# A gated linear-recurrence and retention layer: long gated units in two parts, and the forward forget logits made in the pair products

## The chip, the cores and the metric

The kernel runs on one core of one Trainium2 chip. The metric is device time in microseconds (us) of one execution. The engines are TensorE (PE: matmuls, with weight loads shown as PEld), VectorE (DVE), ScalarE (ACT), GpSimd (POOL) and SyncE (SP, which issues transfers). Each works through its own queue in the order of the program, and waits on semaphores of the others.

## The reference

Two inputs, 512 and 1024 rows of width 1024, pass through the same layer. It projects, runs two kinds of two-way recurrence in chunks, gates, projects again and normalises:

```
u    = x * (1 + scale) + shift                # from silu(c) @ w_ada
proj = u @ w_in                               # aq, af_f, af_b, ai, ag | rq, rk, rv, rg
q_a = silu(aq) * 128**-0.5 ; v_a = ai
forget(fl): logf = logaddexp(log_lb, log1m_lb + log_sigmoid(fl)); kk = (1 - lb) * sigmoid(-fl)
o_a = hgrn2(q_a, k_f, logf_f, v_a) + flip(hgrn2(flipped q_a, k_b, logf_b, v_a))   # 8 heads of 128
y_a = rms_norm(o_a) * a_norm_w * silu(ag)
o_r = retention forward + flipped retention   # 8 heads, rope on q and k
y_r = layer_norm(o_r) * silu(rg)
g_a, g_r = split(sigmoid(u @ w_mg + b_mg))
s   = (g_a * (y_a @ w_pa) + g_r * (y_r @ w_pb)) @ w_out
out = layer_norm(ALPHA * x + (1 + gate) * s) * ln_g + ln_b
```

## The kernel before, in words

Every long product is made of three matmuls per block of 128 rows of u, since each fp32 operand is split into a high and a low part in a faster format: ACT copies the high part of a weight block, DVE subtracts for the low part (lines 104 and 113, class `Stream`, which also loads the raw blocks through SP's queue in the order of a list). `gemm_f` (line 364) makes a [128 x 512] result of 24 matmuls of 512 columns, `gemm_t` (line 375) a [128 x 256] one of 24 matmuls of 256 columns.

The short input (512 rows, group 0) comes first, then the long one (group 1). Work goes by units. A gated unit (kind A) of group 1 is one head with two lanes (its two halves of 512 rows), and there are eight; four rotary units (kind R) follow. For a gated unit, `pre_A` makes the products for q and the two forget logits, `mid_A` those for values and gates, and `stages_A` returns a list of short pieces: a first level and levels h = 1, 2, 4, 8, 16, 32, 64 that build the chunk's score matrix and decay the tile X (`lv_small`, `lv_big`; after each level DVE's `update` multiplies halves of X by factors T, and up to level 8 ACT mixes the next keys KM from X), then transposes of keys (`trk`), state updates (`kvs`), outputs per lane (`o_lane`), and normalised, transposed results (`yt_lane`, tiles y and yT, stored by SP). `interleave` runs a generator of long products (the filler) and puts the next stage in whenever its credit says so; the order in which all this is written is the order of every queue. In group 1, unit i's whole list goes into the products of `mid` of unit i and `pre` of unit i + 1; I call this stretch unit i's slot.

Ahead of the long units, `pair_products` (line 1014; matmuls in line 972) makes two head or gate blocks at a time by a scheme with seven instead of eight half products, 84 matmuls of 512 columns a pair, from sums of u made before (`build_comb`). The list `PAIRED` has twelve gate blocks and, for each segment in `EARLY`, eight heads in four pairs. `EARLY = (0,)` says that q of the long units is made there, written to memory (qd), and read back by `fetch`. `early_g` makes the gates of the rotary units there too.

Of the kernel before, what the change touches and what calls it, by code (L numbers as in the profile page):

```python
# [14 lines left out]
D = 1024  # L15
# [134 lines left out]
def interleave(filler, total, stages, marks, ws, lead=0.0):  # L150

    left = total
    weight = sum(s.w for s in stages)
    i = 0
    credit = -lead
    since = 0.0
    for cost in filler:
        left -= cost
# [25 lines left out]
def layer(ctx, tc, x_p, x_s, c_p, c_s, w_ada, b_ada, w_in, hgrn_lb, a_norm_w, ret_decay, w_pa, w_pb, w_mg, b_mg,  # L184
# [14 lines left out]
    def close_pool():  # L199
# [81 lines left out]
    ]  # L281

    EARLY = (0,)
    FIRST, LAST = range(0), range(12, 16)
# [24 lines left out]
    def order_mid(u):  # L311
        if u.kind == "A":
            for ls in u.wl:
                h = u.lanes[ls[0]][0]
                ws.add("t", (w_in, 3072 + 128 * h), (w_in, 4096 + 128 * h))
        else:
            for base in (6144, 7168)[:2 - u.g]:
                order_vg(u, base)
# [8 lines left out]
    for g in range(2):  # L327
        us = groups[g]
        if g == 0:
            for k in range(NK):  # L330
                ws.add("k", (None, 128 * k))
        else:
            for u in us[8:]:
                order_vg(u, 7168)
# [86 lines left out]
    def pre_A(u):  # L421
        g = u.g
        prep_A(u)
        if g:
            fetch(u)
        for ls in u.wl:
            for seg in [seg for seg in range(3) if g == 0 or seg not in EARLY]:
                j, w = ws.get()
                for l in ls:
                    ps = gbank([128, 512])  # L430
                    yield from gemm_f(ps, w, u_f(g, u.lanes[l][1]))
                    evac(u, l, seg, ps)
                ws.done(j)

    def fetch(u):

        for l in range(2):
# [112 lines left out]
    def stages_A(u):  # L550
        st = []
        for h in (0,) + LEVELS:
            fs = [lv_small(u, l, h) if h <= 16 else lv_big(u, l, h) for l in range(2)]
            st.append(Stage(lambda fs=fs: [f() for f in fs], w=(2.8 if h == 32 else 2.2) if u.g else 2.0))
        steps = kv_steps(u)
# [39 lines left out]

        np_ = len(pairs)
        st.append(Stage(trk(0), w=1.4))
        for n in range(np_):
            if n + 1 < np_:
                st.append(Stage(trk(n + 1), w=0.85 if u.g else 1.0))  # L600
            st.append(Stage(kvs(n), w=0.85 if u.g else 1.0, need=(u, "mid")))
        ys, sss = {}, {}

        def o_lane(l):
            def fn():
# [4 lines left out]
                for c in range(4):  # L610
# [9 lines left out]
                ss = sss[l] = sb("D", [128, 8])  # L620
                for c in range(4):
# [31 lines left out]

        wo = 1.3 if u.g else 1.0
        st += [Stage(o_lane(0), w=wo), Stage(o_lane(1), w=wo), Stage(yt_lane(0)), Stage(yt_lane(1), w=1.5)]
        return st


    def pre_R(u):
        u.X, u.Vt, u.Gt, u.St, u.C = {}, {}, {}, {}, {}  # L660
        for ls in u.wl:
            j, w = ws.get()
            for l in ls:
                b = u.lanes[l][1]
                X = u.X[l] = sb("X", [128, 4, 384])
                for c in range(0, 4, 2):
                    ps = gbank([128, 2, 256])
                    for e in range(2):
                        yield from gemm_t(ps[:, e, :], w, u_t(u.g, b), 128 * (c + e))
                    for e in range(2):  # L670
                        r = 4 * b + c + e
# [40 lines left out]
    def mid_R(u):  # L712
        for part in range(2 - u.g):
            for ls in u.wl:
# [18 lines left out]
            if part == 0:  # L733
                marks.add((u, "v"))
                if u.g:
                    fetch_g(u)
# [10 lines left out]
    def stages_R(u):  # L747
# [4 lines left out]
        def kdec(n):  # L752
            def fn():
                (i, f, _, b, _) = steps[n]
                kt = kds[n] = sb("Kt", [128, 2, 2, 64])
                for d, (l, c) in ((0, f), (1, b)):
# [314 lines left out]
    def pblock(g, b, st):  # L1071
# [4 lines left out]
        def load_g(i):  # L1076
            if i < len(p_order):
                part, n = p_order[i]
                gt[i] = sb(("y", "q")[part], [128, 512], name="gt")
                nc.sync.dma_start(gt[i], gd[g][8 * part + n, :, 512 * b:512 * b + 512])  # L1080
# [5 lines left out]
        for i, (part, n) in enumerate(p_order):  # L1086
# [9 lines left out]
            if part == 0:  # L1096
                t = ta[n] = sb(("Kt", "T2")[n % 2], [128, 512], name="ta")
            else:
# [107 lines left out]
    def load_x(i):  # L1206
        if i < 8:
            for q, tag in ((0, "Kt"), (1, "T2")) if i else ((0, "V"), (1, "G")):
                xt[i, q] = sb(tag, [128, 512], name="xt")
# [247 lines left out]
    PRE = {("A", 0): 31.1, ("R", 0): 20.9, ("A", 1): 31.1 * (3 - len(EARLY)) / 3, ("R", 1): 20.9}  # L1457
    MID = {("A", 0): 20.9, ("R", 0): 41.9, ("A", 1): 20.9, ("R", 1): 20.9}

# [3 lines left out]
    with tc.manual_schedule():  # L1463
        startup()
        more = []
        for g in range(2):
            us = groups[g]
            if g:
                interleave(chain(early_g(us[8]), early_g(us[9])), 41.9, more, marks, ws)
                close_pool()  # L1470
# [5 lines left out]
                open_pool("at1")  # L1476
                run(pre(us[0]))
            for i, u in enumerate(us):
                st = stages_A(u) if u.kind == "A" else stages_R(u)
                if i + 1 < len(us):  # L1480
                    nx = us[i + 1]
                    interleave(chain(mid(u), pre(nx)), MID[u.kind, g] + PRE[nx.kind, g], st, marks, ws, LEAD_IN)
                else:
                    fill = gates(g, LAST) if g else gates(g)
                    interleave(chain(mid(u), fill), MID[u.kind, g] + (41.9 if g else 60.0), st, marks, ws)
            more = []
# [69 lines left out]
```

## Time and profile before

| | |
|---|---|
| runs | 2130.53, 2133.76, 2134.61 us; median 2133.76 |
| profiled execution | 2131.14 us, span 2129.4 us |
| PE busy | 2095.7 us, 98% |
| PEld busy | 1875.5 us, 88% |
| DVE busy | 1212.3 us, 57% |
| ACT busy | 774.5 us, 36% |
| POOL busy | 448.4 us, 21% |

The time of the profiled execution is its span and 1.7 us around it. A matmul's end is modelled, so PE's busy share says that its queue is almost never empty for long, not that it streams all the time; start times tell more.

### The profile page before, as it was taken

How to read it: one execution, taken by the hardware profiler on the slowest of the kernel's cores; microseconds unless marked ns; L12 is line 12 of the kernel's file. 1: busy time of each engine (PE TensorE's matmuls, PEld its weight loads, DVE VectorE, ACT ScalarE, POOL GpSimd, SP SyncE). 2: the span in 40 equal slices, each digit the busy share in tenths (PEclk: the TensorE clock that was granted, in tenths of full speed). 3: DMA queues.
4: the chain of work that ended last, by engine and by line, in shares of the span. 5: the costliest groups of instructions: out<-in, count | busy, mean ns of one | idle time of the engine just before them, and what ended most of it. 6: DMA issues, size and time to landing. Idle time of an engine off the chain costs nothing.

```text
span 2129.4 us, 45909 instructions
## 1 busy us (share of the span) xinstructions
PE 2095.7 (98%) x19211; PEld 1875.5 (88%) x19211; DVE 1212.3 (57%) x2372; ACT 774.5 (36%) x1620; POOL 448.4 (21%) x668
## 2 busy tenths in 40 slices
PE   7999999999999999999999999999999999999997
PEld 5898899998888999887888889888999998889887
DVE  4856764544334858546456665556635654545557
ACT  3644553323322623333344544444421212322221
POOL 3322223321000320000122331322434442100101
PEclk9999999999999999999999999999999999999999
DMA  9322323245775442333311111211222123676752
GB/s 286 110 82 84 96 81 109 70 124 182 234 247 194 140 138 80 114 109 109 105 51 51 61 61 61 71 42 50 62 75 95 60 75 124 220 272 218 235 182 79
DMA packets 336942, 257.78 MB, mean 121 GB/s; under 512 B 10396, under 2 KB 292224, under 8 KB 335712
## 3 DMA queue, kind: packets, MB, share of 16 engines
q1 hardware_dynamic: 324240, 231.84, 34.7%
q10 hardware_dynamic: 11552, 20.98, 2.6%
q8 instruction: 151, 2.47, 0.5%
q0 software_dynamic: 944, 2.02, 0.3%
q14 instruction: 55, 0.45, 0.1%
HBM read 201.32 MB, written 53.49 MB: 120 GB/s over the span
## 4 chain that ended last, share of the span: by engine, by line
PE 89%; DVE 4%; ACT 2%; issue 2%; DMA 1%; POOL 1%; SPq 0%; ACTq 0%; DVEq 0%; POOLq 0%
PE g L375 35%; PE g L364 31%; PE g L972 7%; PE l L618 2%; PE l L506 2%; PE t L581 2%; DVE X L490 2%; PE l L535 1%; PE l L845 1%; PE l L843 1%; PE t L779 1%; PE g L1390 1%; PE t L565 1%; PE t L810 1%; PE l L1390 1%
## 5 line engine op out<-in xcount | busy, mean ns | idle before, releaser
L375 PE MATMUL g<-wh,u 128*128 128x256 f32 x3840 | 733.5, 287 | 0.0
L375 PEld LDWEIGHTS g<-wh,u 128*128 128x128 f32 x3840 | 609.9, 191 | 8.2 <-issue 3.3
L375 PE MATMUL g<-wl,u 128*128 128x256 f32 x1920 | 542.8, 283 | 0.0
L364 PE MATMUL g<-u,w 128*128 128x512 f32 x1776 | 449.6, 400 | 0.0
L364 PEld LDWEIGHTS g<-u,w 128*128 128x128 f32 x1776 | 320.9, 188 | 64.5 <-issue 1.9
L375 PEld LDWEIGHTS g<-wl,u 128*128 128x128 f32 x1920 | 367.7, 192 | 0.0
L364 PE MATMUL g<-y,w 128*128 128x512 f32 x1152 | 261.9, 389 | 0.0
L364 PEld LDWEIGHTS g<-y,w 128*128 128x128 f32 x1152 | 216.0, 188 | 44.9
L113 DVE TENSOR_TENSOR w<-raw,w 128x1024 fp32r<-128x1024 f32 (+2 forms) x134 | 157.6, 1178 | 126.4 <-ACT w L104 126.1
L490 DVE TENSOR_TENSOR X<-X,T 128x512 f32<-128x512 f32 x336 | 219.9, 701 | 3.3 <-PE l L535 2.2
L492 POOL TENSOR_TENSOR T<-T 128x512 f32<-128x512 f32 (+6 forms) x168 | 122.3, 754 | 333.0 <-DVE T L397 331.1
L104 ACT ACTIVATE w<-raw 128x1024 fp32r<-128x1024 f32 (+2 forms) x134 | 134.5, 1013 | 143.0 <-DMA raw<-in_w_pb 36.1
L113 DVE TENSOR_TENSOR wl<-raw,wh 128x1024 fp32r<-128x1024 f32 x96 | 122.5, 1289 | 48.7 <-ACT wh L104 47.5
L104 ACT ACTIVATE wh<-raw 128x1024 fp32r<-128x1024 f32 x104 | 107.0, 1056 | 40.5 <-PE g L375 34.2
L972 PE MATMUL g<-c,w 128*128 128x512 f32 x480 | 112.9, 390 | 1.0 <-DVE u L998 1.0
L375 PE MATMUL g<-wh,sl 128*128 128x256 f32 x384 | 109.9, 286 | 0.0
L375 PE MATMUL g<-wh,sh 128*128 128x256 f32 x384 | 108.6, 283 | 0.0
L375 PE MATMUL g<-wl,sh 128*128 128x256 f32 x384 | 108.6, 283 | 0.0
L972 PEld LDWEIGHTS g<-c,w 128*128 128x128 f32 x480 | 89.9, 188 | 20.9 <-DVE u L998 2.3
L522 POOL COPY A<-D 32x128 f32<-32x128 f32 x96 | 61.9, 645 | 208.2 <-DVE D L515 205.2
L479 ACT ACTIVATE KM<-X 128x256 f32<-128x256 f32 x120 | 51.7, 431 | 108.7 <-DVE X L490 104.1
L972 PE MATMUL g<-u,w 128*128 128x512 f32 x360 | 85.6, 391 | 1.5 <-ACT u L989 1.1
(231 smaller groups left out, 2745.1 us busy)
## 6 DMA issues: line engine op xcount, KB each, us to landing
raw<-in_w_in SPq DMA_DIRECT2D x122, 512.0 KB, 4.0
yd<-yT SPq DMA_DIRECT2D x96, 256.0 KB, 2.2
y<-yd SPq DMA_DIRECT2D x24, 1024.0 KB, 8.3
raw<-in_w_mg SPq DMA_DIRECT2D x36, 512.0 KB, 3.8
raw<-in_w_pa SPq DMA_DIRECT2D x24, 512.0 KB, 4.5
raw<-in_w_pb SPq DMA_DIRECT2D x24, 512.0 KB, 3.8
gt<-gd SPq DMA_DIRECT2D x48, 256.0 KB, 4.2
raw<-in_w_out SPq DMA_DIRECT2D x24, 512.0 KB, 3.9
```

The source lines that it names most:

```text
L104: self.nc.scalar.activation(out=hi, in_=raw, func=AF.Copy)
L113: self.lo.tensor_tensor(out=lo, in0=raw, in1=hi.bitcast(F32), op=ALU.subtract)
L364: T.matmul(ps, w[wi][:, k, :], a[ai](k), start=n == 0, stop=n == 3 * NK - 1)
L375: T.matmul(ps, a[ai](k, t0), w[wi][:, k, :], start=k == 0 and n == 0, stop=k == NK - 1 and ai == wi)
L479: S.activation(out=K4[:, :, 0, :], in_=halves(u.X[l][:, 0, :], h)[:, :, 0, :], func=AF.Copy)
L490: V.tensor_tensor(out=v, in0=v, in1=f, op=ALU.mult)
L492: G.tensor_tensor(out=T2, in0=Tv[:, :, :, 0], in1=Tv[:, :, :, 1], op=ALU.mult)
L506: T.matmul(ps[32 * i:32 * i + 32, c, :], km[:, c0:c0 + 32], qq, start=True, stop=True, tile_position=(0, 32 * i))
L522: G.tensor_copy(out=A[32 * i:32 * i + 32, :, 32 * i:32 * i + 32], in_=u.Dt[l][32 * i:32 * i + 32, :, :])
L581: T.matmul(ps[:, m, :], kt[:, m, :], u.Vt[l][:, c, :], start=True, stop=True)
L618: T.matmul(ps[:, c, :], a, b, start=i == 0, stop=i == len(mm) - 1)
L972: T.matmul(ps, w[wi][:, k0 + k, :], a[ai][:, k, :], start=first and n == 0, stop=n == 11, skip_group_check=True)
```

## The change

`EARLY` becomes (0, 1): the forward forget logits of the eight long gated units are made in four more pairs, stored to fd, fetched into X by SP at the start of `pre_A`, and turned into sigmoids by ACT in the new function `spread` after the unit's first product. `stages_A` returns two lists, levels (first) and the rest (second). In group 1 `merge` puts the second list of unit i - 1 and the levels of unit i into one slot, in the order and with the weights of the table `MERGED`. A filler can now yield a mark, (unit, "free"), at which `interleave` runs stages until that unit's outputs are issued, so that its X may be written again. Tiles V and G get four buffers; Kt and the gates share the buffers of y and yT. Of the rotary units, the first now makes its gates in its own `mid_R` and not ahead of the pairs.

```
     for cost in filler:
+        if isinstance(cost, tuple):
+            while cost not in marks:
+                weight -= stages[i].w
+                stages[i].fn()
+                i += 1
+            continue
...
-            "D": 2, "A": 2, "V": 3, "G": 3, "sg": 2, "Kt": 2, "S": 2, "y": 2, "yT": 2}
+            "D": 2, "A": 2, "V": 4, "G": 4, "sg": 2, "ss": 2, "S": 2, "y": 2, "yT": 2}
...
+    for i, u in enumerate(groups[1]):
+        u.early = u.kind == "R" and i > 8
+        u.before = groups[1][i - 2] if i > 1 and groups[1][i - 2].kind == "A" else None
...
-    EARLY = (0,)
+    EARLY = (0, 1)
...
     def pre_A(u):
         g = u.g
         prep_A(u)
-        if g:
+        n = 0
+        if g and 1 in EARLY:
+            if u.before:
+                yield u.before, "free"
             fetch(u)
...
                     yield from gemm_f(ps, w, u_f(g, u.lanes[l][1]))
+                    if g and n == 0:
+                        if 1 in EARLY:
+                            spread(u)
...
+    def spread(u):
         for l in range(2):
             for seg in (1, 2):
                 if seg in EARLY:
                     ip, im = ((2, 0), (1, 3))[seg - 1]
                     X = u.X[l]
                     S.activation(out=X[:, im, :], in_=X[:, ip, :], func=AF.Sigmoid, scale=-1.0)
                     S.activation(out=X[:, ip, :], in_=X[:, ip, :], func=AF.Sigmoid)
...
-                kt = kts[n] = sb("Kt", [128, 4, 128])
+                kt = kts[n] = sb("y", [128, 4, 128], name="Kt")
...
+        first, st = st, []
...
+                if l == 1:
+                    marks.add((u, "free"))
...
+        return first, st
+
+    def merge(second, first):
+
+        st = []
+        for x, w in MERGED:
+            s_ = first[LV[x]] if x in LV else second[x]
+            s_.w = w
+            st.append(s_)
+        return st + [Stage(lambda: None, w=0.8)]
+
+    LV = dict(zip("dabcefgh", range(8)))
+
+    MERGED = [(0, 0.6), (1, 0.6), (2, 0.6), ("d", 1.0), (3, 0.8), (4, 0.8), ("a", 1.0), (5, 0.8), (6, 0.8),
+              ("b", 1.0), (7, 0.8), (8, 1.3), ("c", 1.0), (9, 1.0), ("e", 1.2), (10, 1.0), ("f", 1.4), (11, 1.0),
+              ("g", 1.8), ("h", 1.8)]
...
-        for part in range(2 - u.g):
+        for part in range(1 if u.early else 2):
...
+                    first, later = stages_A(u)
+                    if g == 0:
+                        st = first + later
+                    else:
+                        st = merge(second, first) if second else first
+                        second = later
+                else:
+                    st = second + stages_R(u)
+                    second = []
```

In `MERGED`, d is the first level, a, b, c, e, f, g, h are levels 1, 2, 4, 8, 16, 32, 64; 0 to 7 are trk and kvs, 8 and 9 the outputs, 10 and 11 the transposed results.

How this moves instructions late in a slot: first PE, from level 16 on in a unit of before (l is the level's bank, line 506 a small level, 535 a big one; g are the long products).

```order
L506 MATMUL l<-X,KM 32x32 x32
L375 MATMUL g<-wh,u 128x256
L375 MATMUL g<-wl,u 128x256
L375 MATMUL g<-wh,u 128x256 x2
L375 MATMUL g<-wl,u 128x256
L375 MATMUL g<-wh,u 128x256 x2
L375 MATMUL g<-wl,u 128x256
L375 MATMUL g<-wh,u 128x256 x2
L375 MATMUL g<-wl,u 128x256
L375 MATMUL g<-wh,u 128x256
L364 MATMUL g<-u,w 128x512 x12
L535 MATMUL l<-X 32x32 x32
```

Twelve products of 512 columns and level 64 (line 535 with 64 columns) follow. Of the change, PE from level 8 to level 64 of one unit (533 and 562 are the levels, 672 the transposes of yt_lane of the unit before).

```order
L533 MATMUL l<-X,KM 32x32 x32
L378 MATMUL g<-u,w 128x512 x6
L672 MATMUL t<-ident,y 128x128 x4
L378 MATMUL g<-u,w 128x512 x12
L533 MATMUL l<-X,KM 32x32 x32
L378 MATMUL g<-u,w 128x512 x6
L672 MATMUL t<-ident,y 128x128 x4
L378 MATMUL g<-u,w 128x512 x12
L562 MATMUL l<-X 32x32 x32
L378 MATMUL g<-u,w 128x512 x12
L562 MATMUL l<-X 64x64 x16
```

The levels 8, 16, 32 and 64 now stand among the 512-column products of the next unit's `pre_A`, with 18, 18 and 12 of them between, and the transposes of the unit before stand there too.

Then DVE between level 16 and level 32's update of X, first in a unit of before (515 is the masked copy of a level, 490 the update with T, 469 the gate, 113 a weight's low part).

```order
L515 COPY_PREDICATED D<-mask,l 128x128
L490 TENSOR_TENSOR X<-X,T_14809 128x32x16 x2
L515 COPY_PREDICATED D<-mask,l 128x128
L490 TENSOR_TENSOR X<-X,T_14834 128x32x16 x2
L469 TENSOR_TENSOR G<-g,sg 128x256
L113 TENSOR_TENSOR wl<-raw,wh 128x8x128
L490 TENSOR_TENSOR X<-X,T_14883 128x16x32 x2
L490 TENSOR_TENSOR X<-X,T_14910 128x16x32 x2
```

And of the change, in the same place (542 and 517 are the copy and the update, 678 is yT's low part of the unit before; 408, 411 and 414 are the start of the next unit's lane 0).

```order
L113 TENSOR_TENSOR wl<-raw,wh 128x8x128
L542 COPY_PREDICATED D<-mask,l 128x128
L517 TENSOR_TENSOR X<-X,T_15646 128x32x16 x2
L542 COPY_PREDICATED D<-mask,l 128x128
L517 TENSOR_TENSOR X<-X,T_15671 128x32x16 x2
L113 TENSOR_TENSOR wl<-raw,wh 128x8x128
L678 SCALAR_TENSOR_TENSOR yT<-t,vec,yT 128x512
L408 TENSOR_TENSOR KM<-X 128x512
L411 TENSOR_SCALAR T_15811<-X,oml,lbm 128x512 x2
L414 TENSOR_TENSOR X<-T_15811,q 128x512 x2
L113 TENSOR_TENSOR w<-raw,w 128x1024
L517 TENSOR_TENSOR X<-X,T_15749 128x16x32 x2
```

Between the update of level 16 (128x32x16) and that of level 32 (128x16x32) there stood a gate and a weight part; now there stand a weight part, a yT part, the four start instructions and another weight part.

Last ACT in the same stretch, first of before (466 and 468 are a value copy and a gate's sigmoid, 104 a weight's high part, 538 a level's copy, 412 and 413 a forget logit's sigmoids).

```order
L466 ACTIVATE V<-g 128x256
L468 ACTIVATE sg<-g 128x256
L104 ACTIVATE wh<-raw 128x8x128
L538 ACTIVATE A<-l 32x4x32 x8
L104 ACTIVATE wh<-raw 128x8x128
L538 ACTIVATE A<-l 64x4x64 x4
L412 ACTIVATE X<-g 128x512
L413 ACTIVATE X<-g 128x512
```

And of the change (663 is the norm of y, 677 yT, 479 and 480 are `spread`, 426 the first sigmoid of the product just made).

```order
L493 ACTIVATE V<-g 128x256
L495 ACTIVATE sg<-g 128x256
L104 ACTIVATE wh<-raw 128x8x128
L663 ACTIVATE y<-y,ss 128x128 x4
L677 ACTIVATE yT<-t,vec 128x512
L104 ACTIVATE wh<-raw 128x8x128
L677 ACTIVATE yT<-t,vec 128x512
L479 ACTIVATE X<-X 128x512
L480 ACTIVATE X<-X 128x512
L479 ACTIVATE X<-X 128x512
L480 ACTIVATE X<-X 128x512
L426 ACTIVATE X<-g 128x512
```

The norm, both yT and the four sigmoids of `spread` now stand ahead of the sigmoids of the next unit's lane 0.

## Rows read from the trace of the kernel before

**Rows 1.** Windows view, one unit: PE, PEld, DVE, ACT, POOL busy, clock, DMA.
```profile
1215.70:1279.90 64.20, 63.94 (x864) 57.15 (x862) 38.19 (x74) 30.81 (x84) 16.40 (x26) 1.00 0.19 59
```
**Rows 2.** Timeline of PE ahead of unit 0: start, length, engine, line, tiles, count.
```profile
1039.80 8.32 PE L364 MATMUL g<-u,w 128*128 128x512 f32 x36
1047.96 0.28 PE L375 MATMUL g<-wh,u 128*128 128x256 f32 x1
...
1049.87 0.28 PE L375 MATMUL g<-wl,u 128*128 128x256 f32 x1
```
**Rows 3.** View of line 972: shortest, median and longest ns, first and last start.
```profile
L972 PE MATMUL g<-u,w x360: 387/389/500, 831.2 to 1026.0; 128*128 128x512 f32 x180
```
**Rows 4.** Timeline of PE in one long gated unit.
```profile
1171.87 1.64 PE L364 MATMUL g<-u,w 128*128 128x512 f32 x6
1173.35 0.60 PE L642 MATMUL t<-ident,y 128*128 128x128 f32 x4
1173.70 1.64 PE L364 MATMUL g<-u,w 128*128 128x512 f32 x6
...
1195.10 0.46 PE L506 MATMUL l<-X,KM 128*32 128x32 f32 x32
...
1196.30 0.39 PE L375 MATMUL g<-wh,u 128*128 128x256 f32 x1
...
1199.36 0.76 PE L506 MATMUL l<-X,KM 128*32 128x32 f32 x64
1200.05 0.39 PE L375 MATMUL g<-wh,u 128*128 128x256 f32 x1
...
1203.11 0.76 PE L506 MATMUL l<-X,KM 128*32 128x32 f32 x64
...
1208.87 3.04 PE L364 MATMUL g<-u,w 128*128 128x512 f32 x12
1211.84 1.15 PE L535 MATMUL l<-X 128*64 128x64 f32 x32
```
**Rows 5.** Timeline of DVE in the same unit.
```profile
1165.61 0.69 DVE L394 TENSOR_TENSOR KM<-X 128x512 f32<-128x512 f32 x1 [1.30 <-ACT X L413]
...
1167.13 1.28 DVE L400 TENSOR_TENSOR X<-T,q 128x512 f32<-128x512 f32 x2
...
1176.58 0.75 DVE L648 SCALAR_TENSOR_TENSOR yT<-t,vec,yT 128x512 fp32r<-128x512 f32 x1 [2.57 <-ACT yT L647]
...
1203.65 0.30 DVE L515 COPY_PREDICATED D<-mask,l 128x128 f32<-128x128 uint8 x1 [0.86 <-PE l L506]
...
1206.65 0.41 DVE L469 TENSOR_TENSOR G<-g,sg 128x256 f32<-128x256 f32 x1
1207.18 1.33 DVE L113 TENSOR_TENSOR wl<-raw,wh 128x1024 fp32r<-128x1024 f32 x1
1208.77 2.70 DVE L490 TENSOR_TENSOR X<-X,T 128x512 f32<-128x512 f32 x4 [0.26 <-PE l L535]
```
**Rows 6.** Timeline of ACT in the same unit; in brackets idle time and releaser.
```profile
1174.69 1.28 ACT L633 ACTIVATE y<-y,D 128x128 f32<-128x128 f32 x4 [1.40 <-POOL D L627]
1175.88 0.67 ACT L647 ACTIVATE yT<-t,vec 128x512 fp32r<-128x512 f32 x1
1180.02 0.69 ACT L647 ACTIVATE yT<-t,vec 128x512 fp32r<-128x512 f32 x1 [3.46 <-DMA yd<-yT]
1180.60 0.59 ACT L412 ACTIVATE X<-g 128x512 f32<-128x512 f32 x1
...
1202.82 0.42 ACT L480 ACTIVATE KM<-X 128x256 f32<-128x256 f32 x1
1205.54 0.38 ACT L466 ACTIVATE V<-g 128x256 f32<-128x256 f32 x1 [2.30 <-PE g L375]
...
1206.08 1.06 ACT L104 ACTIVATE wh<-raw 128x1024 fp32r<-128x1024 f32 x1
```
**Rows 7.** List of transfers: count, size, median us from issue to landing.
```profile
q<-qd SPq DMA_DIRECT2D x16, 256.0 KB, 4.6
```

More of the change, by code (lines that the diff above doesn't have):

```diff
@@ L157, in interleave @@
     for cost in filler:
+        if isinstance(cost, tuple):
+            while cost not in marks:
+                assert stages[i].need is None or stages[i].need in marks
+                weight -= stages[i].w
+                stages[i].fn()
+                i += 1
+            continue
         left -= cost
@@ L281, in layer @@
     ]
-    EARLY = (0,)
+    for i, u in enumerate(groups[1]):
+        u.early = u.kind == "R" and i > 8
+        u.before = groups[1][i - 2] if i > 1 and groups[1][i - 2].kind == "A" else None
+    for u in groups[0]:
+        u.early, u.before = False, None
+    EARLY = (0, 1)
     FIRST, LAST = range(0), range(12, 16)
@@ L316, in order_mid @@
         else:
-            for base in (6144, 7168)[:2 - u.g]:
+            for base in (6144, 7168)[:1 if u.early else 2]:
                 order_vg(u, base)
@@ L332, in layer @@
         else:
-            for u in us[8:]:
-                order_vg(u, 7168)
+            for u in us:
+                if u.early:
+                    order_vg(u, 7168)
             for n in FIRST:
@@ L431, in pre_A @@
                     yield from gemm_f(ps, w, u_f(g, u.lanes[l][1]))
+                    if g and n == 0:
+                        if 1 in EARLY:
+                            spread(u)
+                        else:
+                            if u.before:
+                                yield u.before, "free"
+                            fetch(u)
+                    n += 1
                     evac(u, l, seg, ps)
@@ L553, in stages_A @@
             fs = [lv_small(u, l, h) if h <= 16 else lv_big(u, l, h) for l in range(2)]
-            st.append(Stage(lambda fs=fs: [f() for f in fs], w=(2.8 if h == 32 else 2.2) if u.g else 2.0))
+            st.append(Stage(lambda fs=fs: [f() for f in fs], w=2.0))
         steps = kv_steps(u)
@@ L599, in stages_A @@
             if n + 1 < np_:
-                st.append(Stage(trk(n + 1), w=0.85 if u.g else 1.0))
-            st.append(Stage(kvs(n), w=0.85 if u.g else 1.0, need=(u, "mid")))
+                st.append(Stage(trk(n + 1)))
+            st.append(Stage(kvs(n), need=(u, "mid")))
         ys, sss = {}, {}
@@ L618, in fn @@
                         T.matmul(ps[:, c, :], a, b, start=i == 0, stop=i == len(mm) - 1)
+                if l == 1:
+                    marks.add((u, "free"))
                 junk = sb("sg", [128, 4, 128])
-                ss = sss[l] = sb("D", [128, 8])
+                ss = sss[l] = sb("ss", [128, 8])
                 for c in range(4):
@@ L664, in pre_R @@
                 b = u.lanes[l][1]
-                X = u.X[l] = sb("X", [128, 4, 384])
                 for c in range(0, 4, 2):
@@ L669, in pre_R @@
                         yield from gemm_t(ps[:, e, :], w, u_t(u.g, b), 128 * (c + e))
+                    if c == 0:
+                        if l == 0 and u.before:
+                            yield u.before, "free"
+                        X = u.X[l] = sb("X", [128, 4, 384])
                     for e in range(2):
@@ L734, in mid_R @@
                 marks.add((u, "v"))
-                if u.g:
+                if u.early:
                     fetch_g(u)
@@ L754, in fn @@
                 (i, f, _, b, _) = steps[n]
-                kt = kds[n] = sb("Kt", [128, 2, 2, 64])
+                kt = kds[n] = sb("y", [128, 2, 2, 64], name="Kt")
                 for d, (l, c) in ((0, f), (1, b)):
@@ L1078, in load_g @@
                 part, n = p_order[i]
-                gt[i] = sb(("y", "q")[part], [128, 512], name="gt")
+                gt[i] = sb(("yT", "q")[part], [128, 512], name="gt")
                 nc.sync.dma_start(gt[i], gd[g][8 * part + n, :, 512 * b:512 * b + 512])
@@ L1096, in pblock @@
             if part == 0:
-                t = ta[n] = sb(("Kt", "T2")[n % 2], [128, 512], name="ta")
+                t = ta[n] = sb(("y", "T2")[n % 2], [128, 512], name="ta")
             else:
@@ L1207, in load_x @@
         if i < 8:
-            for q, tag in ((0, "Kt"), (1, "T2")) if i else ((0, "V"), (1, "G")):
+            for q, tag in ((0, "yT"), (1, "T2")) if i else ((0, "V"), (1, "G")):
                 xt[i, q] = sb(tag, [128, 512], name="xt")
@@ L1457, in layer, with mid_cost @@
     PRE = {("A", 0): 31.1, ("R", 0): 20.9, ("A", 1): 31.1 * (3 - len(EARLY)) / 3, ("R", 1): 20.9}
-    MID = {("A", 0): 20.9, ("R", 0): 41.9, ("A", 1): 20.9, ("R", 1): 20.9}
+    def mid_cost(u):
+        return 20.9 if u.kind == "A" or u.early else 41.9
     def run(gen):
@@ L1468, in layer @@
             if g:
-                interleave(chain(early_g(us[8]), early_g(us[9])), 41.9, more, marks, ws)
+                interleave(early_g(us[9]), 20.9, more, marks, ws)
                 close_pool()
@@ L1477, in layer @@
                 run(pre(us[0]))
+            second = []
             for i, u in enumerate(us):
-                st = stages_A(u) if u.kind == "A" else stages_R(u)
+                if u.kind == "A":
+                    first, later = stages_A(u)
[4 more added lines that the diff above has]
+                        second = later
+                else:
+                    st = second + stages_R(u)
+                    second = []
                 if i + 1 < len(us):
                     nx = us[i + 1]
-                    interleave(chain(mid(u), pre(nx)), MID[u.kind, g] + PRE[nx.kind, g], st, marks, ws, LEAD_IN)
+                    interleave(chain(mid(u), pre(nx)), mid_cost(u) + PRE[nx.kind, g], st, marks, ws, LEAD_IN)
                 else:
                     fill = gates(g, LAST) if g else gates(g)
-                    interleave(chain(mid(u), fill), MID[u.kind, g] + (41.9 if g else 60.0), st, marks, ws)
+                    interleave(chain(mid(u), fill), mid_cost(u) + (41.9 if g else 60.0), st, marks, ws)
             more = []
```

4 lines of the change are left out of this document (1 added, 3 removed).

## Prediction

> **What bounds the kernel now.** I read the page first (its first part stands in the table above): TensorE (PE) is busy 98% of the span, VectorE (DVE) 57%, ScalarE (ACT) 36%. So only two things can move the time: less work in PE's queue, or more or fewer waits of that queue. Then I read the stages one by one. The long gated units repeat every 64.2 us; in such a stretch PE shows 63.94 busy out of 64.20, DVE 38.19, ACT 30.81 [rows 1]. "Busy" hides short waits, because a matmul's end is modelled, so I went on by start times. A 512-column product starts every 0.2267 us (36 of them from 1039.80 to 1047.96) and a 256-column one every 0.119 us (16 of them from there to 1049.87) [rows 2]. Ten pair products of 84 matmuls each run from 831.2 to 0.2 behind 1026.0: 195.0 us, 19.5 a pair [rows 3]. In the timeline of PE in one unit [rows 4] the reader is to see three things: the price of each piece of the queue, that level 4 waits between its two lanes (1195.10 to 1196.30 is 1.20 us, where level 8 takes 0.69), and that level 32 and level 64 do not wait at all. Last come DVE and ACT in the same unit [rows 5, 6], because PE waits for them there.
>
> **The work that goes.** Per long unit 48 products of 512 columns leave (forward logits, two lanes of 24): 8 x 48 x 0.2267 = 87.1 us [rows 2]. Four pairs come: 4 x 19.5 = 78.0 us, with their own small waits inside, since the price is start to start [rows 3]. Net -9.1 us.
> The Trainium skill, "TensorE: Matmul & The Clock Gate", section "Back-to-back issue gap", gives N/2.4 + 2.5 ns at full clock for a matmul with nothing beside it, 216 ns at 512 columns; its second figure there, 131 ns for a sustained stream, is far from this trace, which has 227 ns. By 216 ns the net of 48 matmuls would be -10.4 us, by 131 ns -6.3 us. I keep the rows.
>
> **The waits that go.** Levels of one unit stood 24 products of 256 apart, 3.06 us (1200.05 to 1203.11); now two short stages and 24 to 36 such products lie between them, 5 us or more. The wait of 1.20 - 0.69 = 0.5 us for the mixed keys goes: 8 x 0.5 = -4.1 us [rows 4]. Unit 1's slot is the first with merged stages; unit 0's has levels alone, 36 products apart, and does not wait either.
>
> **What is added to PE's queue.** Changing between long products and a stage costs 3.06 - 24 x 0.119 = 0.20 us among 256-column products, and 1.48 - 6 x 0.2267 = 0.12 us among 512-column ones (1171.87 to 1173.35) [rows 4]. Nine stages a slot move from the second kind of place to the first, and one more stop is made: 9 x 0.08 + 0.20 = 0.9 us, in seven merged slots +6.3 us. The half of a gate unit's products that moves from ahead of the pairs into unit 8 is the same work in another place: 0. Buffers with a new tag (Kt in y, gt in yT) are free long before they are asked for: 0; at worst the first gate load of the last blocks waits for one store (about 3.5 us from the first yT's end to the second's start [rows 6]), behind a 24-matmul product of 5.4 us.
>
> **Where a new wait arises.** Level 64 of a unit needs level 32's update of X on DVE. In the order of before, DVE does level 16's updates, one product with a gate, one weight split, and then that update. In the order of the change, the same stretch of DVE also holds both yT halves of the unit before, a second weight split, the whole start of the next unit's lane 0 (KM, T1, X) and a third split, and PE's queue there is no longer: two transposes and 30 products of 512 columns from level 16 to level 64. DVE and ACT work through their queues in order, so all of it comes before level 32's update. I work one slot out, t = 0 at PE's start of level 8.
> PE, if nothing waits: level 0.69, 6 products 1.48, transposes 0.35 (1173.35 to 1173.70), 12 products 2.97 (1208.87 to 1211.84) [rows 4]. Level 16 at 5.49, level 32 at 10.98, level 64 at 14.64.
> DVE and ACT: DVE starts a level 0.54 after PE (1203.11 to 1203.65) and needs 3.0 for both lanes (to 1206.65) [rows 4, 5]: level 8 ends at 3.54. ACT, in its order: last KM copy 0.42, V and sg 0.54, a weight part 1.06, the norm 1.28, yT 0.67 [rows 6]: 7.5. DVE stands before the yT remainder until then: 0.75, split 1.33, and only then level 16: 9.6 to 12.6, not at 6.0. So level 32 waits for lane 1 till 12.6: 1.3 us, and level 64 is due at 15.9. DVE goes on with a split 1.33 and yT 0.75: 14.7. ACT may write the second yT only when the first one's store has landed, 3.47 us on (1176.55 to 1180.02): 11.0, ends 11.7; then four new sigmoids, some 0.5 each, and the two of the evacuation: 15.0 [rows 6]. KM, T1 and X of the next unit take 2.80 (1165.61 to 1168.41): 17.8; the third split 19.1; level 32's update 2.70 for both lanes [rows 5]: 20.5 and 21.8. Level 64 waits 4.6 for lane 0 and another 0.8 for lane 1. Together 6.7; neighbours on one engine start some 0.09 before the one ahead ends (1174.69 + 1.28 against 1175.88), six times in this chain: 6.2 us a slot.
> Bounds: if nothing stood ahead of level 16, DVE would still have 3.0 + 1.33 + 0.75 + 2.8 + 1.33 + 1.35 = 10.6 us of work from 6.0 on, lane 0 at 16.6 against 14.64, and 0.8 for lane 1: 2.3 with the overlaps taken off. Upwards, a weight load late by one landing (4.6 us [rows 7], but most of it beside DVE's own work) adds 2: 8.5. I take 6.2, since every piece has its row. Slots of units 1 to 6 have this form; unit 0's lacks yT and the norm, and by the same steps waits 4 us (2 to 5 by the bounds); unit 7's is followed by a rotary unit, has 36 and 24 products of 256 columns between these levels, and waits for nothing. Sum 6 x 6.2 + 4 = +41.2 us, by the bounds +15 to +56.
> Behind level 64 the wait ends: 36 products follow before the next stage that needs X, and DVE has caught up by then.
>
> **Sum.** -9.1 - 4.1 + 6.3 + 41.2 = +34.3 us on the profiled execution's own 2131.14 us: 2165.4. The median of the runs shown is 2.6 us above that execution, inside their spread of 4 us, so I add nothing for it and say 2165; 0.2% (4 us) is about what a measurement of this kernel can tell from no change. The likeliest case's own range, by the bounds of the new wait, is 2139 to 2180.
>
> **Rivals.**
> *The slots even out (other side).* DVE has 38.2 - 1.2 = 37 us of work in a slot of 64.2 - 10.9 = 53 us, ACT 31: neither is full [rows 1]. If the two hold up PE by no more than the few tenths that before shows, the sum is -9.1 - 4.1 + 6.3 = -6.9 us: 2124. With 41.2 us worth 6.6 slots of 6.2, it decides at 6.9/6.6 = 1.0 us a slot; below that the kernel is faster, below 0.4 measurably. Against it: the load lies unevenly, 10.6 us of DVE work between two points of PE's queue that are 8.6 us apart at DVE's side (6.0 to 14.64), and the bound above is 2.3. Chance 0.14.
> The Trainium skill, "Perfetto Trace Analysis", section "Optimization Strategy", says that where the most contended engine changes over time, interleaving the regimes may help; by that rule the change should land here. No run so far shows it.
> *Waits of about the size of the gain.* 0.4 to 1.6 us a slot, somewhat under the lower bound, if DVE began level 16 at once and the evacuation of lane 0 came a little later than level 32: 2127 to 2135. Chance 0.08.
> *The fetched logits come late.* Four loads per unit are issued as the unit's first product starts, behind the release of X by the outputs of two units before; a load of this size lands in 4.6 us at the median [rows 7], and is needed about 10 us after its issue. If SP's queue holds them 6 us longer (yT's stores wait there for ACT and DVE), the sigmoids, and with them the whole end of the chain, move by 2 us or more in 7 slots: 2165 + 14 = 2179. Chance 0.10, inside "slower".
> *The pairs cost more.* Four more pairs in a row with a copy and two stores from ACT each; if each waited 2 us more than now: +8, 2173. Chance 0.05, likewise.
> The forecast itself: 0.63.
>
> **How the numbers follow.** Slower by over 0.2%: 0.63 + 0.10 + 0.05 = 0.78; within: 0.08; faster: 0.14. The range from 2127 to 2181 takes in the middle cases and leaves out most of the faster one below and a twentieth above.
>
> **What would show it.** Right: slots of units 1 to 6 of 64.2 - 10.9 - 0.5 + 0.9 + 6.2 = 59.9 us; a wait of PE at level 64's first product of 4 to 5 us, released by DVE's update of X, and one of about 1 us at level 32's second lane; 14 pairs in 273 us; no wait for KM at levels 1 to 16. Wrong: a slot of 53.5 us with levels 32 and 64 running through; DVE idle ahead of KM of the next unit for more than the yT wait; or a wait at the first 512-column product's evacuation, which would point to the fetched logits.

## The result, and the profile after

The changed kernel takes 2165.63 us (median of 4 runs, 2163.95 to 2168.73); the kernel before, on the same chip, 2132.15 us (4 runs, 2130.28 to 2134.61). The ratio is 1.0162, with a 95% interval of 1.0150 to 1.0175: slower by 33 us, where 2165 was forecast. The profiled execution is the 2168.73 us one, the slowest of the four.

The view of waits of PE in the changed kernel (line waited at, releaser: us in total, times, longest):

```profile
PE l L562 <- DVE X L517: 36.8, 17, 4.4
PE g L378 <- DMA y<-yd: 4.1, 1, 4.1
```

The first row is levels 32 and 64 (line 562) waiting for DVE's update of X (line 517). The second is a wait near the end that the forecast had put at nothing. The windows view of the changed kernel shows one merged slot and a stretch inside another (columns as in [rows 1]):

```profile
1321.44:1382.25 60.81, 55.29 (x816) 50.92 (x815) 37.84 (x73) 29.41 (x83) 18.64 (x28) 0.94 0.20 62
1192.50:1199.30 6.80, 5.83 (x49) 5.59 (x50) 6.10 (x11) 2.60 (x6) 0.19 (x1) 0.50 0.28 77
```

Against [rows 1] a slot lost 3.4 us, not the 10.9 us of products taken out of it, and PE is idle for 5.5 us of it. The sixth number behind the length is the mean clock. It was 1.00 in [rows 1] and is 0.94 in this slot. In the second row, 6.8 us around the start of level 64 in an earlier slot (at 1193.38, below), it is 0.50: that is 1.2 GHz, where the slots of before had 2.4 GHz.

PE late in one slot (timeline; level 16 is line 533, levels 32 and 64 line 562), to be read against the last lines of [rows 4]:

```profile
1178.58 0.76 PE L533 MATMUL l<-X,KM 128*32 128x32 f32 x64
...
1184.08 0.46 PE L562 MATMUL l<-X 128*32 128x32 f32 x32
1185.55 0.46 PE L562 MATMUL l<-X 128*32 128x32 f32 x32 [1.01 <-DVE X L517]
1185.94 3.02 PE L378 MATMUL g<-u,w 128*128 128x512 f32 x12
1193.38 2.32 PE L562 MATMUL l<-X 128*64 128x64 f32 x32 [4.42 <-DVE X L517]
1195.64 0.58 PE L389 MATMUL g<-wh,u 128*128 128x256 f32 x1
```

DVE in the same stretch, against the last three lines of [rows 5]:

```profile
1180.53 0.75 DVE L678 SCALAR_TENSOR_TENSOR yT<-t,vec,yT 128x512 fp32r<-128x512 f32 x1 [2.26 <-ACT yT L677]
1181.20 1.22 DVE L113 TENSOR_TENSOR wl<-raw,wh 128x1024 fp32r<-128x1024 f32 x1
1182.33 0.29 DVE L542 COPY_PREDICATED D<-mask,l 128x128 f32<-128x128 uint8 x1
...
1185.33 1.31 DVE L113 TENSOR_TENSOR wl<-raw,wh 128x1024 fp32r<-128x1024 f32 x1
1186.56 0.74 DVE L678 SCALAR_TENSOR_TENSOR yT<-t,vec,yT 128x512 fp32r<-128x512 f32 x1
1187.22 0.68 DVE L408 TENSOR_TENSOR KM<-X 128x512 f32<-128x512 f32 x1
1187.82 0.99 DVE L411 TENSOR_SCALAR T<-X,oml,lbm 128x512 f32<-128x512 f32 x2
1188.73 1.31 DVE L414 TENSOR_TENSOR X<-T,q 128x512 f32<-128x512 f32 x2
1189.97 1.21 DVE L113 TENSOR_TENSOR w<-raw,w 128x1024 fp32r<-128x1024 f32 x1
1191.11 3.33 DVE L517 TENSOR_TENSOR X<-X,T 128x512 f32<-128x512 f32 x4
```

DVE stands idle for ACT's yT until 1180.53 and from there works without a pause. Level 16, ready on PE at 1178.58, is copied from 1182.33 on, 3.75 us later; in [rows 5] it was 0.54. Level 32's update starts at 1191.11, when PE has been ready for level 64 since 1188.96 (1193.38 - 4.42). This is the chain of the forecast, piece by piece. (The start of the next unit's lane 0, lines 408, 411 and 414, is five instructions, not the four named above.) The idle time that ends for DVE at 1180.53 comes from ACT (timeline; norm, yT, a weight part, second yT behind the first one's store), as in [rows 6]:

```profile
1178.65 1.27 ACT L663 ACTIVATE y<-y,ss 128x128 f32<-128x128 f32 x4
1179.82 0.68 ACT L677 ACTIVATE yT<-t,vec 128x512 fp32r<-128x512 f32 x1
...
1182.92 0.69 ACT L677 ACTIVATE yT<-t,vec 128x512 fp32r<-128x512 f32 x1 [1.47 <-DMA yd<-yT]
```

Last, the end. SP's queue in the changed kernel (gt is the gate tile that now lies in yT's buffers, yd<-yT the stores it must wait for, y<-yd the last blocks' input):

```profile
1881.04 7.64 SPq L932 DMA_DIRECT2D yd<-yT  x4
1889.65 1.16 SPq L1127 DMA_DIRECT2D gt<-gd  x2
...
1893.49 5.20 SPq L1127 DMA_DIRECT2D gt<-gd  x1
1898.74 1.79 SPq L1114 DMA_DIRECT2D y<-yd  x2
```

And PE there:

```profile
1903.64 2.88 PE L378 MATMUL g<-y,w 128*128 128x512 f32 x12
1910.65 6.71 PE L378 MATMUL g<-y,w 128*128 128x512 f32 x17 [4.13 <-DMA y<-yd]
```

17 products take 6.71 us, where at 0.227 [rows 2] they would take 3.9: the clock is at half here too, until 1916.1.

### The profile page after: what moved, and what is told of

Read it like the earlier page. It is cut to its first block, busy times and chain, and to the rows that moved or that the text cites. A ratio compares the mean times of both kernels' runs of the same rounds, so it can differ in the third digit from the quotient of the medians.

```text
span 2166.8 us, 45884 instructions
## 1 busy us (share of the span) xinstructions
PE 2096.2 (97%) x19163; PEld 1881.6 (87%) x19163; DVE 1248.7 (58%) x2416; ACT 783.1 (36%) x1636; POOL 458.7 (21%) x668
## 4 chain that ended last, share of the span: by engine, by line
PE 83%; DVE 9%; ACT 3%; issue 2%; DMA 2%; POOL 0%; SPq 0%; ACTq 0%; DVEq 0%; POOLq 0%
PE g L389 36%; PE g L378 22%; PE g L1019 10%; DVE X L517 3%; PE l L646 2%; PE l L533 2%; PE t L608 2%; PE l L562 1%; PE l L892 1%; PE l L890 1%; PE t L826 1%; PE g L1437 1%; PE t L592 1%; PE l L1437 1%; PE t L857 1%
## 5 line engine op out<-in xcount | busy, mean ns | idle before, releaser
L389 PE MATMUL g<-wh,u 128*128 128x256 f32 x3840 | 756.0, 290 | 0.0
L389 PEld LDWEIGHTS g<-wh,u 128*128 128x128 f32 x3840 | 620.8, 194 | 8.6 <-issue 3.3
L389 PEld LDWEIGHTS g<-wl,u 128*128 128x128 f32 x1920 | 372.3, 194 | 0.0
L378 PE MATMUL g<-u,w 128*128 128x512 f32 x1392 | 349.9, 400 | 0.0
L378 PEld LDWEIGHTS g<-u,w 128*128 128x128 f32 x1392 | 252.4, 188 | 53.0 <-issue 1.9
L517 DVE TENSOR_TENSOR X<-X,T 128x512 f32<-128x512 f32 x336 | 227.3, 722 | 4.8 <-POOL T L519 3.3
L519 POOL TENSOR_TENSOR T<-T 128x512 f32<-128x512 f32 (+6 forms) x168 | 137.1, 840 | 402.3 <-DVE T L411 400.5
L1019 PE MATMUL g<-c,w 128*128 128x512 f32 x672 | 158.1, 390 | 1.4 <-DVE u L1045 1.4
L1019 PEld LDWEIGHTS g<-c,w 128*128 128x128 f32 x672 | 125.8, 188 | 29.1 <-DVE u L1045 3.1
L1019 PE MATMUL g<-u,w 128*128 128x512 f32 x504 | 119.7, 390 | 1.6 <-ACT u L1036 1.1
L1019 PEld LDWEIGHTS g<-u,w 128*128 128x128 f32 x504 | 94.1, 188 | 23.1 <-ACT u L1036 3.7
```

What stands on the lines that cost most here:

```text
L378: T.matmul(ps, w[wi][:, k, :], a[ai](k), start=n == 0, stop=n == 3 * NK - 1)
L389: T.matmul(ps, a[ai](k, t0), w[wi][:, k, :], start=k == 0 and n == 0, stop=k == NK - 1 and ai == wi)
L517: V.tensor_tensor(out=v, in0=v, in1=f, op=ALU.mult)
L519: G.tensor_tensor(out=T2, in0=Tv[:, :, :, 0], in1=Tv[:, :, :, 1], op=ALU.mult)
L1019: T.matmul(ps, w[wi][:, k0 + k, :], a[ai][:, k, :], start=first and n == 0, stop=n == 11, skip_group_check=True)
```

## The experiments

Theory 1 is the forecast's: DVE's queue, in program order, holds PE late in a slot. Rival 2 is that ACT's sigmoids on the fetched logits (`spread`) do it; rival 3 that putting two units in one slot costs by itself. Slot lengths are from one unit's first trk to the next one's. Each kernel was timed against the kernel before on one chip.

| kernel | median us (runs) | ratio to before, 95% |
|---|---|---|
| changed | 2165.63 (4) | 1.0162, 1.0150 to 1.0175 |
| next start later | 2135.18 (8) | 1.0022, 1.0012 to 1.0033 |
| gate tiles exchanged | 2163.79 (4) | 1.0156, 1.0141 to 1.0171 |
| pairs alone | 2188.31 (4) | 1.0267, 1.0252 to 1.0283 |
| merge alone | 2128.75 (10) | 0.9991, 0.9982 to 1.0000 |
| yT last | 2151.18 (4) | 1.0092, 1.0074 to 1.0109 |
| all three | 2136.72 (11) | 1.0025, 1.0016 to 1.0034 |
| POOL in place of the sigmoids | 2175.15 (2) | 1.0206, 1.0187 to 1.0224 |
| loads in place of the sigmoids | 2165.86 (2) | 1.0161, 1.0143 to 1.0180 |
| second table | 2119.26 (5) | 0.9943, 0.9931 to 0.9956 |
| merge alone, start later, tiles | 2122.36 (5) | 0.9954, 0.9940 to 0.9968 |
| wait filled with products | 2153.40 (4) | 1.0102, 1.0086 to 1.0119 |

### The next unit's start later

```diff
-            if seg == 2:
+            if seg == 2 and u.g == 0:
                 init_lane(u, l)
+            elif seg == 2 and l == 1:
+                init_lane(u, 0)
+                init_lane(u, 1)
```

> The start of the next unit's lane 0 on DVE (KM, T1, X: 2.8 us) is moved from ahead of level 32's update to behind level 64's update; nothing else changes. Theory 1 (DVE's queue late in the slot holds PE at levels 32 and 64, and the half clock follows that wait): the wait at level 64 falls from 4.8 us to about 2 us in each merged slot, level 32's lane 1 keeps its 1.2 us; slots of 59.5 to 60.8 become 57.2 if the half clock stays, about 55 if it goes with the wait: 7 slots, 2166 - 20 = 2146 down to 2129. Rival 2 (ACT's four sigmoids on fetched logits hold the chain): no change, 2163 to 2168. Rival 3 (putting two units in one slot costs by itself, whatever DVE does): no change either.

2135.18 us, 30 us less than the changed kernel for one group of DVE instructions moved. PE at levels 32 and 64 of this kernel (timeline):

```profile
1296.33 0.46 PE L565 MATMUL l<-X 128*32 128x32 f32 x32 [1.01 <-DVE X L520]
1296.72 3.04 PE L378 MATMUL g<-u,w 128*128 128x512 f32 x12
1301.40 0.69 PE L565 MATMUL l<-X 128*64 128x64 f32 x16 [1.65 <-DVE X L520]
1302.61 0.69 PE L565 MATMUL l<-X 128*64 128x64 f32 x16 [0.53 <-DVE X L520]
```

Level 64 waits 1.65 + 0.53 us instead of 4.4 (1.3 to 1.65 and some 0.5 us in five slots, 0.4 us in the sixth), level 32 as in the changed kernel: theory 1. Rival 3 is out as the main cause. Rival 2 would have to hold DVE at the next unit's KM, and in the changed kernel DVE goes into KM at 1187.22 without a wait; the edit alone does not exclude it, and two more kernels below test it. Slots are 54.0 to 57.2 us; of the half-clock stretches, which in the changed kernel's six slots are four of 6.8 us and two of 3.4, two of 3.4 are left.

### The gate tiles exchanged

```diff
-                gt[i] = sb(("yT", "q")[part], [128, 512], name="gt")
+                gt[i] = sb(("q", "yT")[part], [128, 512], name="gt")
```

> Only the buffers of the gate tiles of the last blocks are exchanged (first half in q's, second half in yT's). Theory 1: the wait of 4.1 us for the load of y near 1907 us goes, and the half clock behind it (6.8 us at half speed, 3.4 us lost): 2166 - 7 = 2159, slots unchanged. Rival: the loads of y are late for another reason (the store of y's last part itself), then no change: 2164 to 2167.

The wait and the half clock at the end are gone, and in the profile the stretch from the first y product to the last matmul is 266.52 us, against 273.26 in the changed kernel and 266.28 before. SP's queue in this kernel, then PE:

```profile
1894.61 2.09 SPq L1127 DMA_DIRECT2D gt<-gd  x1
1896.75 2.04 SPq L1114 DMA_DIRECT2D y<-yd  x2
```

```profile
1901.77 13.55 PE L378 MATMUL g<-y,w 128*128 128x512 f32 x58
```

The gate load holds SP 2.09 us instead of 5.20, and PE runs through. The median fell by only 1.8 us where 7 was expected, less than the runs of either kernel spread, and against the kernel before, timed beside each, from +33.5 to +33.1 us. (The start-up ahead of the pairs also differs by some 2 us from one profile to the next.) So 6.7 us is the difference of two executions, one of them the slowest of its kernel. The seven other kernels that keep the tiles as changed wait 0.9 to 2.5 us for y, with a stretch of 267.4 to 270.7 us; the three others with the tiles exchanged do not wait, with 266.4 to 266.7. That the tiles make the wait is shown; that it costs 6.7 us in a usual execution is not.

### The pairs alone, and the merge alone

The first keeps `EARLY = (0, 1)` but gives each unit its own slot with the stage weights of before (`st = first + later`); the second keeps `merge` but has `EARLY = (0,)`.

> The forward forget logits stay in the pairs, but units are not merged: states and outputs first, then the levels, as before. Theory 1 in its wider form (a slot shorter by 10.9 us of products no longer covers the chain of levels): levels stand 12 or 24 products of 256 columns apart instead of 24, where 24 already waited 0.5 us at level 4; each gap of 12 waits 1.5 to 2 us more, some 5 to 7 us a slot, in 8 slots +40 to +56, less 9.1 for the products and about 0 to 7 for the end: 2165 to 2185. Rival 3 (the merge is what costs): about 2132 - 9 + 7 = 2130. Rival 2 (the fetched logits hold the chain): the wait stands at the first level or at lane 0's start, not in between the levels.

> Units are merged, but the forward forget logits are made in the slots as before (48 products of 512 columns more in a slot than in the changed kernel). Theory 1: PE has 10.6 us from level 16 to level 64 where DVE needs about 9.3 us, so level 64 waits 0 to 1 us; slots of 64 to 65.5 us; the end keeps its 7 us: 2134 to 2146, no half clock in the slots. Rival 2 (fetched logits): no wait at all at level 64, 2132 to 2137. Rival 3 (the merge costs by itself): a wait of 4 us or more at level 64 as in the changed kernel, slots of 68 us or more, 2160 and over.

The pairs alone take 2188.31 us, worse than with the merge and 3 us over what was written. Rival 3 is out: without the merge the same shorter slots are longer, 61.0 to 63.7 us. But the place was half missed. PE's waits in this kernel:

```profile
PE l L646 <- DVE S L617: 20.4, 7, 3.0
PE l L533 <- ACT KM L507: 14.8, 19, 1.0
PE t L672 <- ACT y L663: 8.5, 7, 1.2
```

Only the second row, with some 0.5 us at level 64, is the waits between levels, 2.6 us a slot and not 5 to 7. The larger one is the outputs (line 646) waiting for DVE's states S, some 3 us a slot, with a half-clock stretch behind it in five of seven slots. In this order a slot of some 53 us does not hold one unit's states, outputs and levels one after the other: the pairs are 23 us dearer without the merge than with it. That no other order would do is not shown.

The merge alone comes to 2128.75 us. PE of this kernel, same place:

```profile
1326.16 0.76 PE L562 MATMUL l<-X 128*32 128x32 f32 x64
1326.85 3.04 PE L378 MATMUL g<-u,w 128*128 128x512 f32 x12
1330.19 0.69 PE L562 MATMUL l<-X 128*64 128x64 f32 x16 [0.30 <-DVE X L517]
1331.39 0.69 PE L562 MATMUL l<-X 128*64 128x64 f32 x16 [0.52 <-DVE X L517]
```

Both sides of the balance differ here. With longer slots 24 products of 512 columns lie between levels 16 and 32 in place of 18, 1.4 us more room (6 x 0.2267); and on DVE one weight part of 1.3 us stands between level 16's copy and level 32's update where the changed kernel has two there and a third ahead of the copy, while the lane start is still ahead of the update. That spares level 32's 1.0 us and nearly all of level 64's 4.4. It is faster than was written because slots are 64.3 us, at the low end, and the end lost 3.75 us and not 7.

### The sigmoids of the fetched logits left out, twice

```diff
-                            spread(u)
+                            for x in range(2):
+                                G.memset(u.X[x][:, 0:3:2, :], 0.25)
```

> The four sigmoids of the fetched logits are left out (POOL fills the two planes of X with a constant in their place, so the forward forget gates of the long units are not made). Rival 2 (these sigmoids hold the chain): the wait at level 64 goes or falls by 2 us or more, 2150 or less. Theory 1: DVE does not wait for ACT at the next unit's KM; the wait at level 64 stays within 0.5 us of 4.8 us, 2160 to 2168.

It got slower, which neither theory had said, and it settles nothing about ACT: the fill itself went into the chain. DVE of this kernel, ahead of the next unit's KM (a line of its timeline):

```profile
1192.85 0.69 DVE L408 TENSOR_TENSOR KM<-X 128x512 f32<-128x512 f32 x1 [1.70 <-POOL X L452]
```

1.70 us of waiting for POOL, and level 64 waits up to 6.2 us instead of 4.4: a delay ahead of level 32's update is paid in full. The second form leaves `spread` out and lets two more loads write the second plane.

> The four sigmoids of the fetched logits are left out (the second plane is filled by two more loads of the logits, so the forward forget gates of the long units are not made), with POOL left as it is in the changed kernel. Rival 2: the wait at level 64 falls by 2 us or more, 2150 or less. Theory 1: DVE does not wait for ACT ahead of the next unit's KM, the wait at level 64 stays within 0.5 us of 4.8 us: 2160 to 2168.

2165.86 us, and in PE's waits:

```profile
PE l L563 <- DVE X L518: 30.8, 12, 4.5
```

The longest is 4.5 us, as with the sigmoids. Rival 2 is out.

### yT last, and all three edits

```diff
-              ("e", 1.2), (10, 1.0), ("f", 1.4), (11, 1.0), ("g", 1.8), ("h", 1.8)]
+              ("e", 1.2), ("f", 1.4), ("g", 1.8), ("h", 1.8), (10, 1.0), (11, 1.0)]
```

> Only the table of the merged order changes: the two yT stages of the unit before (their norm and copies on ACT, 0.75 us each on DVE, with DVE's 2.3 us of idle time before the first) stand behind level 64 and no longer at levels 16 and 32; level 32's update then comes in DVE's queue ahead of the next unit's lane 0 as well. Theory 1: DVE has level 32's update done before PE gets to level 64; the waits of 1.2 and 4.8 us and the half clock go in the six slots of units 1 to 6, each 53.5 to 55 us; unit 0's slot (wait and half clock) and the end stay: 2166 - 6 x 5.8 = 2131, 2127 to 2136. Rival 2 (the fetched logits' sigmoids on ACT hold the chain): these stand as before, so the waits stay: 2160 and over. Rival 3 (the merge costs by itself): no change.

> The yT stages last, both lanes of the next unit started behind level 64's update, and the gate tiles exchanged. Theory 1: as yT last, and unit 0's slot loses its wait and half clock (6 us less in total), the end 7 us: 2131 - 4 - 7 = 2120, 2115 to 2124, below the kernel before by 0.3 to 0.8%. Against it: DVE now has both starts (5.6 us) and both yT parts behind level 64; if the first level of the next unit waits for KM, 1 to 2 us a slot come back: 2127 to 2133.

Both missed, 2151 (four runs, 2145.88 to 2155.17) and 2137. The new order also brought level 32 nearer to level 16: only 12 products of 512 columns lie between them. PE with yT last (1236.12 is level 16), then DVE:

```profile
1236.12 1.05 PE L533 MATMUL l<-X,KM 128*32 128x32 f32 x64
1237.10 3.03 PE L378 MATMUL g<-u,w 128*128 128x512 f32 x12
1241.05 0.46 PE L562 MATMUL l<-X 128*32 128x32 f32 x32 [0.92 <-DVE X L517]
1242.55 0.46 PE L562 MATMUL l<-X 128*32 128x32 f32 x32 [1.03 <-DVE X L517]
```

```profile
1238.19 1.23 DVE L113 TENSOR_TENSOR wl<-raw,wh 128x1024 fp32r<-128x1024 f32 x1 [0.53 <-ACT wh L104]
1239.33 0.29 DVE L542 COPY_PREDICATED D<-mask,l 128x128 f32<-128x128 uint8 x1
```

A weight part that waits for ACT still stands ahead of level 16's copy, so level 32 waits 1.95 us now in both lanes. I had counted the work that I moved, and not the room that moved with it.

### A second table, and the merge alone with the other two edits

The second table has both other edits, and moves the levels up (24 products between levels 16 and 32, 12 between 32 and 64):

```diff
-              ("e", 1.2), (10, 1.0), ("f", 1.4), (11, 1.0), ("g", 1.8), ("h", 1.8)]
+              ("e", 1.2), ("f", 1.4), (10, 1.2), ("g", 2.2), (11, 1.0), ("h", 1.0)]
```

> The kernel of all three edits, but with the yT stages between levels 16 and 32 and levels 32 and 64 again, and the levels moved up: 24 products of 512 columns between levels 16 and 32 (12 before), 12 between 32 and 64. Theory 1 (only the room on PE's queue between two levels against DVE's work in it counts): 6.6 us of PE from level 16 to 32 where DVE needs 3.5, then 4.2 us to level 64 where DVE needs about 3.3 more behind three parts: waits under 0.5 us, no half clock in the slots, six slots of 53.5 to 54.5 us; 2120, 2116 to 2126. Against it (the granted clock falls for other reasons than the wait at these levels): half-clock stretches stay, 2128 to 2135.

> The merged kernel without the four pairs, with both lanes started behind level 64's update and the gate tiles exchanged. Theory 1: against merged units alone (2128.8) the end gives 3.5 us back and the 0.3 to 0.5 us waits at level 64 about 3 us: 2122, 2119 to 2126. Beside the kernel with the second table it shows what the pairs themselves are worth where neither waits: 9.1 us by the sum. If merging gains nothing: 2129 to 2132.

Both came as written: 2119.26 and 2122.36 us. A slot of the second table, by the windows view, and its levels 32 and 64 on PE:

```profile
1299.12:1352.61 53.49, 52.50 (x816) 48.25 (x815) 38.19 (x75) 29.33 (x83) 18.61 (x27) 1.00 0.23 71
```

```profile
1341.86 0.76 PE L565 MATMUL l<-X 128*32 128x32 f32 x64
...
1346.37 0.69 PE L565 MATMUL l<-X 128*64 128x64 f32 x16 [0.33 <-DVE X L520]
1347.58 0.69 PE L565 MATMUL l<-X 128*64 128x64 f32 x16 [0.52 <-DVE X L520]
```

53.5 us in five of six slots (52.4 in the sixth), clock 1.00, with DVE's work in a slot, 38.2 us, the same as before. This kernel beats both. Between their medians lie 3.1 us, where 9.1 was written for the pairs. But that was for two kernels that do not wait, and the second table's still waits at its levels, 5.4 us for DVE's X and 1.5 us for KM, the other 0.7 us in all. With these taken off, the pairs would be worth some 9 us (an estimate; the two tables differ too). Against before, the merge without the pairs is worth 8.8 us, more than the pairs add here.

### The wait filled with products

```diff
+            if h == 64 and l == 0 and u.g and u is not groups[1][7]:
+                a = uh[1, 0, 0]
+                for i in range(18):
+                    T.matmul(ps, a[:, 0, 0:128], a[:, 1, 0:512], start=True, stop=True)
```

> The changed kernel with 18 extra products of 512 columns (4.1 us, their result is overwritten) on PE ahead of level 64's first lane in units 0 to 6, where PE waits 4.4 us in the merged slots and about 3 us in unit 0's. PE gets to the level no earlier and no later, but it works instead of waiting. If the clock falls because PE stood still there: no half-clock stretch behind level 64 in the six merged slots, so the slots of 59.5 to 60.8 us become 57.8 to 58.6 (the wait stays, the half clock's 1.7 to 3.4 us go), 2150 to 2158 in all. If the clock falls for another reason (the long run of matmuls before, the small matmuls of the level): the stretches stay, slots of 59.5 to 61, 2164 to 2172.

2153.40 us: with 18 more products in each of seven slots the kernel is 12 us faster. PE of this kernel, and a slot by windows:

```profile
1363.91 4.24 PE L560 MATMUL l<-u 128*128 128x512 f32 x18
1368.49 0.69 PE L566 MATMUL l<-X 128*64 128x64 f32 x16 [0.34 <-DVE X L517]
```

```profile
1316.23:1374.82 58.59, 56.62 (x835) 51.64 (x833) 37.80 (x74) 29.32 (x83) 18.23 (x27) 1.00 0.21 65
```

The clock is 1.00; no stretch at half is left in any slot. Slots are 58.5 us (57.4 the last), 350.0 in six where the changed kernel has 360.5 and the second table 319.8. So of the 40.7 us that six slots lose, 10.5 are the half clock and 30.1 the wait itself.

## Why the prediction was right, step by step

The place, the releaser and the rough size of the main cost were as written; three terms were off and nearly cancelled, so that 2165 stands so close to 2165.63 is luck in part. Two slips of the working did not carry: from level 16 to level 64 PE has one stop for transposes, not two (the sum has it right), and the upper bound, 6.2 + 2, is 8.2 us a slot and not 8.5, which ends the likeliest range at 2178 and not at 2180.

- **Work that goes.** 14 pairs take 272.3 us (806.4 to 1078.4), 273 were said; four pairs are 77.3, not 78.0.

```profile
L1019 PE MATMUL g<-u,w x504: 387/389/504, 806.4 to 1078.4; 128*128 128x512 f32 x168
```

- **Waits that go.** KM waits in the slots fall to a single one of 0.2 us: right.
- **The sum without the new wait** was -6.9 us. The second table's kernel shows what can be had: -12.0 us at the last matmul, with 6.9 us of waits at the levels still in it. Six slots lose 65.3 us where 63.0 were said (10.6 a slot in most, 11.8 in the last), the pairs 0.7; the other 2 us are ahead of the first slot and behind the sixth, and I have not followed them.
- **The new wait** was 6.2 us a slot and 4 for unit 0, +41.2. Against the second table's kernel six slots lose 6.8 us each (40.7) and unit 0's 4.2. The wait is 5.0 of it (5.4 by the view of waits, which counts from no wait at all), where 6.2 were said; 1.75 is the half clock, which stood nowhere in the forecast. Level 64's 4.4 to 4.8 us (3.8 in the last slot) and level 32's 1.0 are near what was written; the 0.8 us for level 64's second lane came in the last slot (1.36) and hardly elsewhere.
- **The slots:** 59.5 to 60.8 us, 59.9 said.
- **Buffers under new tags** were put at 0, with "at worst the first gate load of the last blocks waits for one store". That step failed: +6.9 us in the profiled execution, 1.2 to 4.4 in the other kernels with these tiles. The gate load did have its time, as said, but it stands in SP's queue ahead of the loads of y, and these were late. Who is queued behind a waiting transfer was not asked.

By the profiles: -12.0 + 44.3 (seven slots and their surroundings) + 6.9 is 39.2, less 1.6 by which the starts of these two executions differ: 37.6, against 37.45 us between the last matmuls of before and after. All terms are differences between the same three traces, so they have to add up; it shows only that nothing was left out. The medians give 33, and the profiled execution of after is its slowest: in a usual one the end probably costs less than 6.9 us, how much was not measured.

Of the rivals, late logits (ACT waits once for them, 0.8 us) and dearer pairs did not come. "The slots even out" did not come either, but its mechanism is real: its point of decision, 1.0 us a slot, is undercut by the second table (0.33 + 0.52 us of waits at level 64, much as in the merge alone), and the kernel is then faster by more than the forecast's 6.9 us. The Trainium skill, "Perfetto Trace Analysis", section "Optimization Strategy", says that interleaving regimes with different limits may help. The runs agree once the order leaves room (0.9954 for the merge without the pairs); in the change as made the same rule did not show.

## What to carry to other kernels

When work is taken out of the bounding engine's queue, look at the shortest distance between two of its dependent steps, and list what the helper's in-order queue holds between the two answers; busy shares (DVE 57%) say nothing about it. Move the helper's work that nobody waits for soon behind the answer that is waited for, then set the distances, and count both again after each move. And when a tile gets other buffers, ask which transfers stand behind its load in the queue, not only when it is needed.

## What the runs showed of the hardware

The granted clock fell to half, 1.2 GHz, during or just behind waits of PE: at level 64, after 3.8 to 4.8 us in a slot, for 3.4 or 6.8 us, and after 4.1 us at the end for 6.8 us. The length of a wait alone does not settle it. With the next start later, two of the five slots that wait 1.3 to 1.65 and then 0.5 us at level 64 have 3.4 us at half, and three have none; with the pairs alone, two of the seven waits of 2.9 to 3.0 us at line 646 left the clock at 2.4 GHz. When the time of the wait was filled with products the clock did not fall in any slot. That is the direct evidence: apart from these products, the matmuls around the wait and their order were unchanged. So a wait costs more than its length here, 6.8 us for 5.0. The Trainium skill, "TensorE: Matmul & The Clock Gate", section "Part 1: The HAM clock gate", says that the gate follows how busy PE has lately been; this agrees. What decides between no fall, 3.4 and 6.8 us was not tested.
